# A hybrid attention layer on one core: the attention phase issued from a list of streams, and later values as transposed blocks

## The chip, the cores and the metric

The kernel runs on one core of one Trainium2 chip. The metric is the device time of one execution in microseconds (us); lower is better. The core's engines run side by side, each with its own instruction stream in a fixed order, and meet at semaphores: TensorE (PE, matrix products, with its weight loads shown as PEld), VectorE (DVE), ScalarE (ACT), GpSimd (POOL) and SyncE (SP), which issues the DMAs.

## The reference

One layer over x of 1024 frames by 1024 features, in float32, with RMS norms around each part:

```python
h = rmsnorm(x, g_mix_pre)
proj = h @ w_in          # fq, fk, fv, f_logit, cq, ck, cv
y_fox = forgetting_attention(fq, fk, fv, f_logit + b_fgt)       # 8 heads of 64
y_chk = chunked_relpos_attention(cq, ck, cv, rel_bias)          # 8 heads of 64
y = concat(rmsnorm(y_fox, g_fox_out), rmsnorm(y_chk, g_chk_out))
x = x + rmsnorm(y @ w_out, g_mix_post)
h = rmsnorm(x, g_mem_pre); mem_n = rmsnorm(mem, g_mem_kv)       # 256 memory tokens
x = x + rmsnorm(memory_cross_attention(h, mem_n, w_mq, w_mk, w_mv, w_mo), g_mem_post)
h = rmsnorm(x, g_ff_pre)
x = x + rmsnorm(square(relu(h @ w_ff1)) @ w_ff2, g_ff_post)
```

Forgetting attention ("f") is causal: query block i of 128 frames sees the i + 1 key blocks up to its own, with a bias from a cumulative sum of log forget gates. Chunked attention ("c") lets a chunk of 64 frames see itself and eight chunks before it, at most five key blocks per query block, with a relative-position bias.

## The kernel before

Every product is made from two parts of each float32 operand: a rounded part ("hi", made by ACT as a copy) and a remainder ("lo", made by DVE or POOL as a subtraction). `mm3` (lines 100 to 104) issues three matmuls for each product: hi x hi, lo x hi and hi x lo. Weights come by DMA into `wraw` (three buffers), and are split into `whi` and `wlo` (two buffers each) by `split_w` (lines 96 and 97).

The kernel has four stages: a prologue that normalises and transposes x into `hT` (two halves of 512 frames, hi and lo) and makes two groups of values; the attention phase; output projection and cross-attention; and the feed-forward part.

The attention phase goes through eight pairs of heads in the order c0, c1, f0, f1, f2, f3, c2, c3. For a pair:

- `project` (lines 261 to 295) makes the key block and then the query block: a stationary 128 x 128 weight block against 512 frames, 48 matmuls of 512 columns for each. Keys are written as `kd` (hi) and `kl` (lo, three buffers of the tag `klo`), and each half of 64 partitions is copied to the other half by a DMA (lines 281 and 283). Queries become `qs`.
- `values` (lines 224 to 235) makes the values of four heads: a stationary 128 x 128 block of `hT` against 256 columns of weights, 24 matmuls per block of frames, 192 for a group. Groups 0 and 1 are made in the prologue, groups 2 (heads f4 to f7) and 3 (c4 to c7) inside the attention phase.
- `attend` (lines 309 to 395), once per head, goes over four groups of two query blocks. It has scores (lines 338 to 342, pieces of up to 512 columns, in two PSUM banks of the tag `s`), the bias added and the row minimum taken by DVE in one instruction (line 344), the exponential by ACT (350), a reciprocal by DVE (352), the row scaled by POOL (353), transposes of the probabilities (379, two banks of `tr`), their split into `ph` by ACT (380) and `pl` by DVE (381), and four matmuls of 256 columns for every two key blocks (386 and 387, two banks of `pv`). The output leaves through `o2` and `ot` (391 and 392) and a DMA to DRAM (`od`).

The memory tokens are normalised during the fourth pair and transposed during the seventh. After the last pair come memory keys (`mem_keys`: 8 weight blocks, 24 matmuls of 256 columns each) and memory values (`mem_values`: 8 weight blocks, 12 matmuls of 512 columns each). Their weight remainders go alternately to DVE and POOL.

The prologue and the main part of the feed-forward stage are inside a block in which the written order is kept. Everything between, the attention phase included, is outside such a block: the compiler's scheduler, which estimates each instruction's duration and issues what is ready by the place in the text, makes the order. The code below is therefore not the order of issue; projections of the next pair and memory products appear between the steps of attention. Once made, each engine's order is fixed. A pool of 31 tiles of 4 KB per partition (`u4`) holds `hT` (16), queries, keys, values and later operands; a tile waits for the last reader of the one that it takes the place of.

Of the kernel before, what the change touches and what calls it, by code (L numbers as in the profile page):

```python
# [5 lines left out]

# [15 lines left out]
P = 128  # L22
# [11 lines left out]
def f(ap):  # L34
    return ap.bitcast(F32)


def layer(tc, out, t):
    nc = tc.nc
    ctx = ExitStack()  # L40
    with ctx:
        build(ctx, tc, nc, out, t)


def build(ctx, tc, nc, out, t):
# [16 lines left out]
    def u4(name, shape, dt=F32R):  # L62

        return up.tile(list(shape), dt, tag="u4", bufs=31, name=name)
# [83 lines left out]
    maskf = up.tile([P, P], F32, tag="u4", bufs=31, name="maskf")  # L148
# [31 lines left out]
    def load_x(b):  # L180
        tag = "sp" if b % 3 else "klo"
        xt = p1.tile([P, D], F32, tag=tag, bufs=5 if b % 3 else 3, name=f"x_{b}")
        nc.sync.dma_start(xt, t["x"][b * P:(b + 1) * P, :])
        return xt
# [6 lines left out]
    def bias_rows():  # L191

        rrow = p1.tile([8, 768], F32, tag="sp", bufs=5, name="rrow")
        rsrc = p1.tile([8, 256], F32, tag="sp", bufs=5, name="rsrc")
        nc.sync.dma_start(rsrc, t["rel_rev"])
        nc.vector.tensor_scalar(rrow[:, 511:767], rsrc, -1.0, None, op0=ALU.mult)
# [6 lines left out]
    def value_weights(g, raws=None, only=None):  # L203

        n = 264 if g == 0 else 256
        src = t["w_v0"] if g == 0 else t["w_v"][g - 1]
# [29 lines left out]

    def forget_gates():

        z, e, l, u = [p1.tile([8, S], F32, tag="sp", bufs=5, name=f"f{n}") for n in "zelu"]
        for g in range(2):  # L240
# [3 lines left out]
            nc.vector.tensor_scalar(z[:, g * HT:(g + 1) * HT], tr.rearrange("p a b -> p (a b)"),  # L244
                                    bfgt, None, op0=ALU.add)
        nc.vector.tensor_scalar(l, z, -1.0, None, op0=ALU.mult)
        nc.vector.tensor_tensor(l, l, z, op=ALU.min)
        nc.scalar.activation(e, l, AF.Exp)

        nc.vector.tensor_scalar(u, e, 1.0, None, op0=ALU.add)  # L250
        nc.scalar.activation(l, u, AF.Ln)
        nc.vector.scalar_tensor_tensor(e, u, 1.0, e, op0=ALU.subtract, op1=ALU.subtract)
        nc.scalar.activation(u, l, AF.Exp, scale=-1.0)
        nc.vector.tensor_tensor(e, e, u, op=ALU.mult)
        nc.vector.tensor_sub(e, e, l)
        nc.vector.scalar_tensor_tensor(e, z, 0.0, e, op0=ALU.min, op1=ALU.add)
        nc.vector.memset(u, 0.0)
        nc.vector.tensor_tensor_scan(l, e, u, 0.0, op0=ALU.add, op1=ALU.add)
        nc.sync.dma_start(cd, l)

    def project(kind, pr):

        qb = (0 if kind == "f" else 8) + pr
        kb = qb + 4
        qs = [u4(f"qs{kind}{pr}{a}", (P, S)) for a in range(2)]
        kd = [u4(f"kd{kind}{pr}{a}", (P, S)) for a in range(2)]
        kl = [p1.tile([P, S], F32R, tag="klo", bufs=3, name=f"kl{kind}{pr}{a}") for a in range(2)]  # L270
        step = 1 if kind == "f" else -1
        halves = [(slice(a * 64, a * 64 + 64), slice(64 - a * 64, 128 - a * 64)) for a in range(2)]
        wh, wl = load_w(t["w_qk"][kb], [P, KC, P])
        for th in range(2):
            ps = mm_tile([P, HT], f"k{kind}{pr}_{th}")
# [3 lines left out]
            for a, (own, oth) in enumerate(halves):  # L279
                nc.scalar.activation(kd[a][own, cs], ps[own], AF.Copy)  # L280
                nc.sync.dma_start(f(kd[a][oth, cs]), f(kd[a][own, cs]))
                nc.vector.tensor_sub(kl[a][own, cs], ps[own], f(kd[a][own, cs]))
                nc.sync.dma_start(f(kl[a][oth, cs]), f(kl[a][own, cs]))
        wh, wl = load_w(t["w_qk"][qb], [P, KC, P])
        for th in range(2):
            ps = mm_tile([P, HT], f"q{kind}{pr}_{th}")
            for kc in range(KC):
                mm3(ps, wh[:, kc, :], wl[:, kc, :], hT[th].hi(kc), hT[th].lo(kc), kc == 0, kc == KC - 1)
            pv = ps.rearrange("p (a b) -> p a b", b=P)[:, :, ::step]
            for a, (own, oth) in enumerate(halves):  # L290
                dst = qs[a].rearrange("p (a b) -> p a b", b=P)[:, th * 4:th * 4 + 4, :]
                nc.scalar.activation(dst[own], pv[own], AF.Copy, scale=-0.125)
                nc.vector.scalar_tensor_tensor(dst[oth], pv[own], -0.125, f(dst[own]),
                                               op0=ALU.mult, op1=ALU.subtract)
        return qs, kd, kl

    def head_bias(kind, h):
        bt = p1.tile([P, S], F32, tag="bias", bufs=2, name=f"bias{kind}{h}")
        if kind == "f":
            nc.sync.dma_start(bt, cd[h:h + 1, :].to_broadcast([P, S]))  # L300
        else:
            row = rd[h:h + 1, :]
            src = bass.AP(tensor=row.tensor, offset=row.offset, ap=[[1, P], [1, 640]])
            nc.sync.dma_start(bt[:, 0:640], src)
            nc.gpsimd.memset(bt[0:64, 0:64], BIG)
            nc.gpsimd.memset(bt[64:128, 576:640], BIG)
        return bt

    def attend(kind, pr, a, qs, kd, kl, vs):
        h = pr * 2 + a  # L310
        hv = (pr % 2) * 2 + a
        own = slice(a * 64, a * 64 + 64)
        oth = slice(64 - a * 64, 128 - a * 64)
        bt = head_bias(kind, h)
        kcol = pr if kind == "f" else 4 + pr
        step = 1 if kind == "f" else -1
        for g in range(4):
            nm = f"{kind}{h}g{g}"
            probs = []
            for i in (2 * g, 2 * g + 1):  # L320
                b0 = 0 if kind == "f" else max(0, i - 4)
                nk = (i + 1 - b0) * P
                k0 = b0 * P
                boff = 0 if kind == "f" else 640 - nk
                if g > 1 or i % 2 == 0:
                    wide = p1.tile([P, S], F32, tag="sp", bufs=5, name=f"sp{nm}{i}")
                sp = wide if g > 1 else wide[:, i % 2 * HT:(i % 2 + 1) * HT]
                mn = small.tile([P, 2], F32, tag="mn", bufs=6, name=f"mn{nm}{i}")
                if nk <= 512:
                    pieces = [(0, nk)]  # L330
                else:
                    first = 512 if nk - 512 >= 256 else nk - 256
                    pieces = [(0, first), (first, nk - first)]
                for j, (o, n) in enumerate(pieces):
                    w = max(n, 256)
                    ps = mm_tile([P, HT], f"s{nm}{i}{j}", "s")
                    last = kind == "f" and j == len(pieces) - 1
                    nc.tensor.matmul(ps[:, :w], qs[a][:, i * P:(i + 1) * P],
                                     kd[a][:, k0 + o:k0 + o + w], start=True, stop=False)
                    if last:  # L340
                        nc.tensor.matmul(ps[:, n - P:n], identb, mask, start=False, stop=False)
                    nc.tensor.matmul(ps[:, :w], qs[a][:, i * P:(i + 1) * P],
                                     kl[a][:, k0 + o:k0 + o + w], start=False, stop=True)
                    nc.vector.tensor_tensor_reduce(
                        out=sp[:, o:o + n], in0=ps[:, :n], in1=bt[:, boff + o:boff + o + n],
                        scale=1.0, scalar=3e38 if j == 0 else mn[:, 0:1],
                        op0=ALU.add, op1=ALU.min, accum_out=mn[:, j:j + 1])
                sm = small.tile([P, 2], F32, tag="sm", bufs=6, name=f"sm{nm}{i}")
                m = mn[:, len(pieces) - 1:len(pieces)]
                nc.scalar.activation(sp[:, :nk], sp[:, :nk], AF.Exp, scale=-1.0, bias=m,  # L350
                                     accum_out=sm[:, 0:1])
# [1038 lines left out]
```

## Time and profile before

| | |
|---|---|
| median of three runs | 1543.71 us (1543.68 to 1544.41) |
| the profiled execution | 1547.0 us, of which the span of its instructions is 1545.2 us |
| mean granted TensorE clock | 0.995 |
| first projection matmul, first output-projection matmul | 66.3 us, 567.8 us |
| HBM traffic over the span | 136 GB/s |

In the rows below, L338 is line 338 of the kernel, a name such as `sf7g<-kdf,qsf` says what is written and from what, with buffer numbers left out (`sf` and `sc` are scores, `ptrf` transposed probabilities, `pvf` the product with values), and a bracket at the end of a row tells for how long the engine stood idle before it and what released it. The duration of a matmul includes its way through the array, which overlaps the next one's, so durations of successive rows overlap.

### The profile page before, as it was taken

How to read it: one execution, taken by the hardware profiler on the slowest of the kernel's cores; microseconds unless marked ns; L12 is line 12 of the kernel's file. 1: busy time of each engine (PE TensorE's matmuls, PEld its weight loads, DVE VectorE, ACT ScalarE, POOL GpSimd, SP SyncE). 2: the span in 40 equal slices, each digit the busy share in tenths (PEclk: the TensorE clock that was granted, in tenths of full speed). 3: DMA queues.
4: the chain of work that ended last, by engine and by line, in shares of the span. 5: the costliest groups of instructions: out<-in, count | busy, mean ns of one | idle time of the engine just before them, and what ended most of it. 6: DMA issues, size and time to landing. Idle time of an engine off the chain costs nothing. (4 is left out here: it accounts for less than half of the span.)

```text
span 1545.2 us, 21983 instructions
## 1 busy us (share of the span) xinstructions
PE 1501.4 (97%) x7852; PEld 1270.6 (82%) x7852; DVE 938.2 (61%) x1640; ACT 789.8 (51%) x1405; POOL 374.2 (24%) x546
## 2 busy tenths in 40 slices
PE   8999999999999999989999998999999999999998
PEld 7978889789878987768888877888888888888886
DVE  6366574665466773775455468676455574746577
ACT  5356564565466675444444455555555544444442
POOL 4234351343234430121011320443233000000021
PEclk9999999999999999999999999999999999999999
DMA  5132140252222454453143154775444595535565
GB/s 215 50 95 66 52 113 23 66 156 64 56 65 90 121 169 139 160 184 106 55 154 105 55 177 168 242 246 181 153 155 150 189 384 194 171 114 192 198 245 191
DMA packets 83856, 220.71 MB, mean 143 GB/s; under 512 B 9865, under 2 KB 13969, under 8 KB 83746
## 3 DMA queue, kind: packets, MB, share of 16 engines
q1 hardware_dynamic: 83746, 219.30, 42.7%
q8 instruction: 62, 1.02, 0.3%
q14 instruction: 48, 0.39, 0.1%
HBM read 159.96 MB, written 50.91 MB: 136 GB/s over the span
## 5 line engine op out<-in xcount | busy, mean ns | idle before, releaser
L96 ACT ACTIVATE whi<-wraw 128x1024 fp32r<-128x1024 f32 x76 | 80.3, 1058 | 76.5 <-PE ym L104 19.0
L1117 ACT ACTIVATE whif<-ra 128x1024 fp32r<-128x1024 f32 x37 | 39.2, 1061 | 122.1 <-PE fy L103 62.6
L1119 DVE TENSOR_TENSOR wlof<-ra,whif 128x1024 fp32r<-128x1024 f32 x37 | 45.3, 1225 | 91.1 <-ACT whif L1117 91.1
L97 DVE TENSOR_TENSOR wlo<-wraw,whi 128x1024 fp32r<-128x1024 f32 x52 | 63.6, 1225 | 53.8 <-ACT whi L96 53.2
L1233 POOL TENSOR_SCALAR rf<-sf 128x1 f32<-128x1 f32 x8 | 8.3, 1035 | 326.5 <-ACT jf L1218 326.2
L102 PE MATMUL v<-whiv,hT_hi 128*128 128x256 f32 (+1 forms) x256 | 73.6, 287 | 1.0 <-DVE vs L235 1.0
L103 PE MATMUL v<-wlov,hT_hi 128*128 128x256 f32 (+1 forms) x256 | 73.2, 286 | 0.0
L104 PE MATMUL v<-whiv,hT_lo 128*128 128x256 f32 (+1 forms) x256 | 73.1, 286 | 0.0
L97 POOL TENSOR_TENSOR wlo<-wraw,whi 128x1024 fp32r<-128x1024 f32 x24 | 57.8, 2410 | 54.2 <-ACT whi L96 28.1
L102 PE MATMUL fx<-vhif,whif 128*128 128x512 f32 x168 | 65.4, 389 | 0.0
L104 PE MATMUL fx<-vhif,wlof 128*128 128x512 f32 x168 | 65.4, 389 | 0.0
L103 PE MATMUL fx<-vlof,whif 128*128 128x512 f32 x168 | 65.4, 389 | 0.0
L1007 POOL TENSOR_TENSOR sc<-wf,wf 128x512 f32<-128x512 f32 x14 | 22.8, 1627 | 144.4 <-DMA wf<-in_w_ff 125.0
L102 PE MATMUL yw<-whi,yT_hi 128*128 128x512 f32 x128 | 51.0, 403 | 2.2 <-ACT yw L605 1.6
L103 PE MATMUL ym<-wlo,oT_hi 128*128 128x512 f32 x128 | 50.9, 397 | 0.9 <-DVE wlo L97 0.8
L103 PE MATMUL mq<-h2T_lo,whi 128*128 128x512 f32 x128 | 51.5, 402 | 0.0
L102 PE MATMUL mq<-h2T_hi,whi 128*128 128x512 f32 x128 | 51.3, 402 | 0.1
L104 PE MATMUL mq<-h2T_hi,wlo 128*128 128x512 f32 x128 | 51.0, 399 | 0.0
L103 PE MATMUL yw<-wlo,yT_hi 128*128 128x512 f32 x128 | 50.6, 395 | 0.1
L102 PEld LDWEIGHTS v<-whiv,hT_hi 128*128 128x128 f32 x256 | 49.1, 192 | 1.5 <-DVE vs L235 1.2
L104 PE MATMUL yw<-whi,yT_lo 128*128 128x512 f32 x128 | 50.3, 393 | 0.0
L104 PE MATMUL ym<-whi,oT_lo 128*128 128x512 f32 x128 | 50.2, 395 | 0.0
(751 smaller groups left out, 5135.5 us busy)
## 6 DMA issues: line engine op xcount, KB each, us to landing
ra<-gd SPq DMA_DIRECT2D x56, 512.0 KB, 3.8
wg<-in_w_ff SPq DMA_DIRECT2D x56, 512.0 KB, 5.6
wf<-in_w_ff SPq DMA_DIRECT2D x38, 512.0 KB, 3.8
gd<-s SPq DMA_DIRECT2D x48, 256.0 KB, 2.1
wraw<-in_w_qk SPq DMA_DIRECT2D x16, 512.0 KB, 4.0
wraw<-in_w_mq SPq DMA_DIRECT2D x16, 512.0 KB, 4.3
wraw<-in_w_mo SPq DMA_DIRECT2D x16, 512.0 KB, 3.8
gd<-u SPq DMA_DIRECT2D x32, 256.0 KB, 2.1
```

The costliest lines, as they stand in the source:

```text
L96: nc.scalar.activation(hi, raw, AF.Copy)
L97: (lo_on or nc.gpsimd).tensor_sub(lo, raw, f(hi))
L102: nc.tensor.matmul(ps, lh, rh, start=start, stop=False, skip_group_check=more)
L103: nc.tensor.matmul(ps, lh, rl, start=False, stop=False, skip_group_check=more)
L104: nc.tensor.matmul(ps, ll, rh, start=False, stop=stop, skip_group_check=more)
L1007: eng.tensor_sub(sc[:, k1], r0[:, k0], r1[:, k0])
L1117: nc.scalar.activation(ah, ra, AF.Copy)
L1119: nc.vector.tensor_sub(al, ra, f(ah))
L1233: nc.gpsimd.tensor_scalar(r, ssf[b][:, 0:1], ssf[b][:, 1:2], EPS, op0=ALU.add, op1=ALU.add)
```

## The change

The attention phase becomes a block with a written order, and that order is computed while the program is built. `Flow` keeps one clock for PE and a time for each of DVE ("V"), ACT ("S"), POOL ("G") and SP's DMAs ("D"), with a duration for each instruction. Five streams are Python generators: each yields the PE time of its next step and a condition. At every point the first stream in the list whose condition holds gives its step; when none does, the clock goes on by 0.05 us. Instructions of the other engines are put in by the time at which they become ready, by level (0 first). `Tokens` count the buffers of each kind.

```python
    def past(self, at):
        return at + 0.2 <= self.now
...
    def run(self, streams):
        heads = [[g, next(g, None)] for g in streams]
        ...
            for h in heads:
                if h[1] and h[1][1]():
                    cost = h[1][0]
                    self.end = self.now + cost + 0.2
                    h[1] = next(h[0], None)
                    self.upto(self.now + cost)
                    ...
                    break
            else:
                ...
                self.upto(self.now + 0.05)
```

```diff
+    free = {k: Tokens(flow, n) for k, n in
+            dict(s=2, tr=2, pv=2, mm=2, sp=1, p=2, klo=4, bias=2, raw=2, w=0, u4=6).items()}
...
+        flow.run([value_steps(), turn_steps(), score_steps(), side_steps(), filler_steps(keep)])
```

The streams are: the products with values (one step for every two key blocks, 0.48 us); the transposes of probabilities; the scores (one piece for a step); side work (the forget gates, the transposes of values, the transposes of memory tokens); and the filler: for each pair the query block, from the fifth pair on the value block, and the key block, each in steps of three matmuls, and after the last pair memory keys and values.

```diff
+    def filler_steps(keep):
+        for n in range(8):
+            part = all_of(("qk", n), 12)
+            yield from project_steps("q", n, part)
+            if n > 3:
+                yield from project_steps("v", n, part)
+            yield from project_steps("k", n, part)
+        for _ in range(16):
+            free["u4"].give(flow.end)
+        yield from memory_steps(keep)
```

A projection may begin when its weight block is split and a bank and its output tiles are free; scores of a pair when its queries, keys and the key copies are complete:

```diff
+                yield (0.681, lambda: kc or there((what, n)) and free["mm"].ready() and
+                       (th or free["u4"].ready(u) and (what != "k" or free["klo"].ready(2))))
...
+                    def then(at, lo=lo, last=last, copy=copy, d=d, l=l):
+                        flow.load(at, lambda: copy(d), part, 2.3)
+                        flow.put("V", at, 0.7, lo, lambda end: (last(end), flow.load(
+                            end, lambda: copy(l), part, 2.3)), 1)
...
+            for what, m in (("u4", 2), ("klo", 1)):
+                for _ in range(m):
+                    free[what].give(flow.end)
```

The last three lines stand at the end of each head's scores.

Values of the last four pairs (f2, f3, c2, c3) are no longer made in groups of four heads. For each of these pairs a block of 128 weight columns is stationary against 512 frames, as for queries and keys; ACT copies the result out (`vt`), TensorE transposes it in blocks of 128, and ACT and DVE split the transposes into the value tiles:

```diff
+                for b in range(4):
+                    nc.tensor.transpose(tr[:, b, :], vt[n][:, th * HT + b * P:th * HT + (b + 1) * P], ident)
...
-        "w_v": a(np.stack([rows(cv[:, :256]), rows(fv[:, 256:]), rows(cv[:, 256:])])),
+        "w_v1": rows(cv[:, :256]),
+        "w_v": blocks(np.concatenate([fv[:, 256:], cv[:, 256:]], 1)),
```

`Stock` loads weight blocks in the order in which they are used and splits them as buffers come free: the rounded part on ACT, the remainder in two halves, on POOL for queries, keys and values and on DVE for memory keys and values:

```diff
+                vec = key[0] in ("mk", "mv")
...
+                def halves(at, key=key, eng="V" if vec else "G"):
+                    cost = 0.61 if eng == "V" else 1.3
```

Three blocks are loaded and two of them split within the prologue's loop, where the small loads for gates and biases also go:

```diff
+            if b == 2:
+                nc.sync.dma_start(bfgt, t["b_fgt"])
+                nc.sync.dma_start(gcol, t["g_heads"])
+                bias_rows(0)
+            if b == 4:
+                bias_rows(1)
+                stock.load(3)
+            if b == 6:
+                stock.split_now(2)
```

The tag `klo` has four buffers instead of three, and `u4` has 30 tiles instead of 31. All instructions after the attention phase are written as before.

More of the change, by code (lines that the diff above doesn't have):

```diff
@@ L35, in f, with __init__, ready, take @@
     return ap.bitcast(F32)
+class Tokens:
+    def __init__(self, flow, n):
+        self.flow, self.free = flow, [0.0] * n
+    def ready(self, n=1):
+        return len(self.free) >= n and sorted(self.free)[n - 1] <= self.flow.now
+    def take(self):
+        self.free.sort()
+        self.free.pop(0)
+    def give(self, at):
+        self.free.append(at)
+class Flow:
+    def __init__(self):
+        self.now = self.end = 0.0
+        self.free = dict.fromkeys(("V", "S", "G", "D"), 0.0)
+        self.waiting = {e: [] for e in self.free}
+        self.count, self.pumps = 0, []
+    def past(self, at):
+        return at + 0.2 <= self.now
+    def put(self, eng, at, cost, call, then=None, level=0):
+        self.count += 1
+        self.waiting[eng].append((level, at, self.count, cost, call, then))
+    def load(self, at, call, then=None, took=4.5):
+        self.put("D", at, 0.55, call, then and (lambda end: then(end + took)))
+    def chain(self, at, parts, then=None, level=2):
+        if not parts:
+            return then and then(at)
+        eng, cost, call = parts[0]
+        more = lambda end: self.chain(end + (2.5 if eng == "D" else 0.05), parts[1:], then, level)
+        self.put(eng, at, cost, call, more, level)
+    def upto(self, t):
+        while True:
+            best = None
+            for e, items in self.waiting.items():
+                if items:
+                    start = max(self.free[e], min(i[1] for i in items))
+                    if start <= t and (best is None or start < best[0]):
+                        best = (start, e)
+            if best is None:
+                break
+            start, e = best
+            item = min(i for i in self.waiting[e] if i[1] <= start)
+            self.waiting[e].remove(item)
+            _, _, _, cost, call, then = item
+            self.free[e] = start + cost
+            call()
+            if then:
+                then(start + cost + 0.05)
+        self.now = t
+    def run(self, streams):
+        heads = [[g, next(g, None)] for g in streams]
+        idle = 0
+        while any(h[1] for h in heads):
+            for pump in self.pumps:
+                pump()
+            for h in heads:
[4 more added lines that the diff above has]
+                    self.upto(self.now + cost)
+                    idle = 0
+                    break
+            else:
+                idle += 1
+                assert idle < 4000, "no step can be taken"
+                self.upto(self.now + 0.05)
+        self.upto(math.inf)
@@ L235, in values, with there @@
         nc.vector.tensor_sub(vs[kb // 2][:, kb % 2, :, 64:128], src, f(dh))
+    ORDER = (("c", 0), ("c", 1), ("f", 0), ("f", 1), ("f", 2), ("f", 3), ("c", 2), ("c", 3))
+    HALVES = [(slice(a * 64, a * 64 + 64), slice(64 - a * 64, 128 - a * 64)) for a in range(2)]
+    flow = Flow()
+    free = {k: Tokens(flow, n) for k, n in
+            dict(s=2, tr=2, pv=2, mm=2, sp=1, p=2, klo=4, bias=2, raw=2, w=0, u4=6).items()}
+    seen = {}
+    def there(*keys):
+        return all(flow.past(seen.get(k, math.inf)) for k in keys)
@@ L252, in forget_gates @@
[L252 to L273, printed above, removed]
+            parts.append(("V", 0.75, lambda g=g, tr=tr: nc.vector.tensor_scalar(
+                z[:, g * HT:(g + 1) * HT], tr.rearrange("p a b -> p (a b)"), bfgt, None, op0=ALU.add)))
@@ new lines, in done @@
+        def done(at):
+            seen["gates"] = at
+            for _ in range(4):
+                free["sp"].give(at)
+        for _ in range(2):
+            free["tr"].take()
+        flow.chain(flow.end, parts[:2], lambda at: [free["tr"].give(at) for _ in range(2)] and
+                   flow.chain(at, parts[2:], done))
+    bias, qs, kd, kl, vs2, probs, trs, pvs = {}, {}, {}, {}, {}, {}, {}, {}
+    heads = [(n, a) for n in range(8) for a in range(2)]
+    units = [(n, a, g) for n, a in heads for g in range(4)]
@@ new lines, in build, with __init__, pump, load @@
+    class Biases:
+        def __init__(self):
+            self.left = list(heads)
+        def pump(self):
+            while self.left and free["bias"].ready():
+                n, a = self.left[0]
+                kind, pr = ORDER[n]
+                if kind == "f" and not there("gates"):
+                    break
+                self.left.pop(0)
+                free["bias"].take()
+                h = pr * 2 + a
+                def load(n=n, a=a, kind=kind, h=h):
+                    bt = bias[n, a] = p1.tile([P, S], F32, tag="bias", bufs=2, name=f"bias{kind}{h}")
+                    if kind == "f":
+                        nc.sync.dma_start(bt, cd[h:h + 1, :].to_broadcast([P, S]))
+                    else:
+                        row = rd[h:h + 1, :]
+                        nc.sync.dma_start(bt[:, 0:640], bass.AP(tensor=row.tensor, offset=row.offset,
+                                                                ap=[[1, P], [1, 640]]))
+                def edges(bt):
+                    nc.gpsimd.memset(bt[0:64, 0:64], BIG)
+                    nc.gpsimd.memset(bt[64:128, 576:640], BIG)
+                if kind == "f":
+                    flow.load(flow.now, load, mark(("bias", n, a)))
+                else:
+                    flow.load(flow.now, load, lambda at, n=n, a=a: flow.put(
+                        "G", at, 0.3, lambda: edges(bias[n, a]), mark(("bias", n, a))))
@@ new lines, in key_steps @@
+    def key_steps(n, g):
+        kind = ORDER[n][0]
+        lo = [block_range(kind, i) for i in (2 * g, 2 * g + 1)]
+        kbs = list(range(lo[0], 2 * g + 2))
+        out = []
+        for c in range(0, len(kbs), 2):
+            slots = [(j, q) for j in range(2) for q in range(2)]
+            outside = lambda: [m for m, (j, q) in enumerate(slots) if not lo[q] <= kbs[c + j] <= 2 * g + q]
+            if outside():
+                slots = slots[2:] + slots[:2]
+            out.append((kbs[c:c + 2], slots, outside()))
+        return out
@@ L279, in project @@
[L279 to L307, printed above, removed]
@@ L397, in raw_tile @@
-    def raw_tile(name):
-        return wp.tile([P, D], F32, tag="wraw", bufs=3, name=name)
+                yield (0.681, lambda: kc or there((what, n)) and free["mm"].ready() and
+                       (th or free["u4"].ready(u) and (what != "k" or free["klo"].ready(2))))
+                if kc == 0:
+                    free["mm"].take()
+                    if th == 0:
+                        for _ in range(u):
+                            free["u4"].take()
+                        if what == "k":
+                            for _ in range(2):
+                                free["klo"].take()
+                    ps = mm_tile([P, HT], f"{what}{n}_{th}")
@@ new lines, in mem_norm, with mem_loads @@
+            store = lambda xt=xt, b=b: nc.sync.dma_start(md[b], xt)
+            flow.chain(flow.now + 6 + b, [("S", 1.1, square), ("G", 0.9, root), ("V", 1.3, scale), ("D", 0.55, store)],
+                       lambda at, b=b: [free["raw"].give(at) for _ in range(1 + b)] and seen.__setitem__(("md", b), at))
+    mem_in = []
+    def mem_loads():
+        for b in range(2):
+            xt = raw_tile(f"memn{b}")
+            nc.sync.dma_start(xt, md[b])
+            mem_in.append(xt)
+        seen["mem"] = flow.now + 6
```

538 lines of the change are left out of this document (369 added, 169 removed).

## The prediction

> **What bounds the kernel now.** I read the page first, then the busy times by stretch, then TensorE's rows in order of time, then the DMA issues.
>
> ```profile
> span 1545.2 us, 21983 instructions
> ...
> PE 1501.4 (97%) x7852; PEld 1270.6 (82%) x7852; DVE 938.2 (61%) x1640; ACT 789.8 (51%) x1405; POOL 374.2 (24%) x546
> ...
> PE 37%; DVE 1%; DMA 1%; issue 0%; ACT 0%; SPq 0%; DVEq 0%; POOLq 0%; POOL 0%; ACTq 0%
> ```
>
> TensorE (PE) sets the end; no other engine is near full. The change touches what runs from the first projection matmul (66.3) to the first output-projection matmul (567.8). In the busy times by stretch (length, then busy time of PE, PEld, DVE, ACT, POOL, then clock and DMA) that phase and three shorter pieces read:
>
> ```profile
> 66.30:567.80 501.50, 487.21 (x3048) 426.24 (x3046) 312.86 (x854) 300.14 (x624) 183.94 (x328) 1.00 0.30 87
> ...
> 350.00:400.00 50.00, 50.00 (x383) 47.27 (x382) 25.05 (x72) 22.89 (x52) 15.16 (x25) 1.00 0.17 51
> ...
> 446.00:463.00 17.00, 13.95 (x89) 11.06 (x88) 14.43 (x47) 13.07 (x30) 7.26 (x16) 1.00 0.35 96
> ...
> 568.00:575.00 7.00, 7.00 (x30) 5.73 (x29) 4.46 (x8) 3.65 (x6) 1.47 (x1) 0.85 0.24 78
> ```
>
> DVE is busy 62% of the phase, ACT 60%, POOL 37%. Busy PE hides gaps, because rows overlap. Undisturbed rows show what a matmul really takes (start, duration):
>
> ```profile
> 379.57 0.28 PE L103 MATMUL v<-wlov,hT_hi 128*128 128x256 f32 x1
> 379.69 0.28 PE L104 MATMUL v<-whiv,hT_lo 128*128 128x256 f32 x1
> ...
> 1400.28 0.39 PE L102 MATMUL fy<-vhif,whif 128*128 128x512 f32 x1
> 1400.51 0.39 PE L103 MATMUL fy<-vlof,whif 128*128 128x512 f32 x1
> ```
>
> From start to start a 512-column matmul takes 0.227 us and a 256-column one 0.120; the same reading gives 0.175 for 384 columns, 0.109 for a transpose, 0.039 for the mask. The phase's instructions by form are 960 of 512 columns, 1340 of 256, 128 of 384, 546 transposes, 64 masks and 8 small sums: 217.9 + 160.8 + 22.4 + 59.5 + 2.5 + 0.9 = 464.0 us of PE work in 501.5. So **37.5 us are gaps**, all that a better order can win here. They are unevenly spread. At 350 to 400, with value projections at hand to fill in, the same sum gives 49.2 of 50: 0.8 us of gaps. At 446 to 463, with attention alone, it gives 11.2 of 17:
>
> ```profile
> 448.68 0.50 PE L338 MATMUL sf7g<-kdf,qsf 128*128 128x512 f32 x1 [0.46 <-DVE mnf7g L344]
> ...
> 450.73 0.28 PE L386 MATMUL pvf7g<-phf7g,vs 128*128 128x256 f32 x1
> 451.85 0.44 PE L338 MATMUL sc4g<-kdc,qsc 128*128 128x384 f32 x1 [0.84 <-DVE mnc4g L344]
> ...
> 456.23 0.55 PE L379 MATMUL ptrf7g<-ident,spf7g 128*128 128x128 f32 x3 [0.85 <-POOL spf7g L353]
> ```
>
> PE stands, first in its order, at a score waiting for a bank that DVE has yet to reduce, or at a transpose waiting for POOL's normalised row, and no projection follows until 467.
>
> [...] By busy time the phase would have 14.3 us to win, by spacing 37.5; I go by spacing.
>
> **The change, part by part.**
>
> *PE work.* Removed: two value groups of 192 matmuls, 384 x 0.120 = 46.1 us. Added: four value blocks of 48 matmuls of 512 columns, 192 x 0.227 = 43.6, and 32 transposes, 3.5. Scores, turns, value products, q and k projections and memory are the same instructions. Net **+1.0 us**.
>
> *Other engines.* Copying a value block out costs ACT 8 copies of 0.60 and 8 splits of 0.60 against 16 of 0.38 (+3.4 us), DVE 8 x 0.69 against 16 x 0.42 (-1.2). The 8 memory-weight remainders that POOL had go to DVE (8 x 1.225 = +9.8 us in the last 80 us, where a memory block gives PE 2.9 us of work and DVE 1.2 + 0.4). Halving the other remainders adds at most 0.1 us x 20 on POOL. All this lies beside PE at 62, 60 and 37% busy; without that cover it would cost 12 us at most. I take nothing.
>
> *DMA and SP.* As many weight loads (512 KB), key copies and bias loads as before, issued in the list's order; SP waits in that order too, so a late key copy holds back weight loads and stores queued behind it. Phase traffic is 87 GB/s. Nothing for bytes.
>
> *The order.* Turn, score and value steps go ahead of projections, and whenever none is expected to be ready one projection step (three matmuls, 0.68 us) is taken. That attacks the gaps above directly. Query blocks now go before key blocks and there is a fourth buffer for key remainders; before, with three, a pair's keys could not be projected until the previous pair's first head let go of one. What is left of the 37.5 us I bound by rows: if all the phase is like 350 to 400, 0.84 x 465/50 = 8 us; if nothing improves, 37.5. The durations written into the list agree with the trace: copy 0.6 against 0.59, remainder 0.7 against 0.69, POOL row multiply 0.25 + 640/1150 = 0.81 against 0.804. One does not, the landing of key copies, written as 2.3:
>
> ```profile
> klc<-klc SPq DMA_DIRECT2D x16, 128.0 KB, 3.9
> ...
> klf<-klf SPq DMA_DIRECT2D x16, 128.0 KB, 2.6
> ```
>
> A pair's first score waits for them, PE stands in order at that score, and the filler queued behind it waits too: 1.6 us at three chunked boundaries and 0.3 at four others, 6 us if nothing covers. So **14 us** of gaps stay, nearer the fed stretch than the starved one, because the memory blocks (45 us) now follow as filler to the end.
>
> *Start.* Before, the value groups covered the wait for the first projection weights: PE has no gap of half a microsecond from 54 to 82. After, three blocks are loaded and two split during the prologue's value matmuls (ACT 2 x 1.06, POOL 4 x 1.2 us). Between -1 and +4 us; I take 0.
>
> *Hand-off.* Before, output-projection weights and head outputs were loaded and split under the memory values, and its first matmuls ran beside the last head. After, attention and memory are one written order, and part of this may come only after the last memory copy: first split 1.06 + 1.2, head outputs 4 x 0.72 on ACT, about 6 us, if not drawn ahead. That code outside a written order can be drawn into it shows at 54.09, where forget-gate transposes run amid the prologue's values. Between -2 (the last head's 3 us of gaps at 563 to 568 go) and +6. One slot fewer in the large pool (30 for 31) may delay a late load by one landing (3.8 us), or not. Together I take **+2 us**.
>
> The row at 568 to 575 shows a price tied to such gaps: clock 0.85, matmuls starting 0.43 us apart, after the thinly filled stretch before it. The Trainium skill (TensorE: Matmul & The Clock Gate, HAM oscillation) warns that idle gaps over about 3.4 us drop the clock to half. Here it fell though no single gap was that long, so a thin stretch suffices; by that rule an empty hand-off would add an estimated 1.7 us to my sum, which also stands within the range.
>
> *Sum.* -37.5 + 1.0 + 14 + 2 = -20.5 us. The profiled execution took 1547.0 us (span 1545.2, 1.8 around it); that gives 1526.5. The median of the runs is 1543.71, so **1523 us**.
>
> **The rivals.**
>
> 1. *Slower: the fine order is late at its waits.* 192 score pieces and 152 value steps each wait for DVE's or ACT's last result. Before, scores and value products have 29.7 us of the gaps ahead of them, 0.086 us for each of 344 places. The list allows 0.2 us for a result to arrive and then fixes the order; a result that comes later holds PE with the projection behind it. Zero gain lies at a residue of 34.5 us, 0.10 us per place; at 0.13 the residue is 45, the change +10, the time 1554. For: PE breaks its runs more often now, and DVE takes two more weight remainders per memory pair. Against: the durations agree, and the prior gaps are mostly where no filler was near.
>
> 2. *Starved at pair boundaries.* The next pair's key block needs two large tiles, which come free when a head's last score is issued. If filler runs out at the seven boundaries and the 446 stretch recurs there (5.9 us of gaps in 17, say half of that more than I counted), 7 x 2 = 14 us more: 1537. For: six large tiles are free at the start, four taken by each pair. Against: the fourth remainder buffer, and value blocks as filler from the fifth pair.
>
> 3. *Nearly all gaps close.* A residue of 4 us and no hand-off cost: 1511.
>
> 4. *The list doesn't set the order.* Code drawn into it displaces its steps, or it ends no better than the order before: residue 32 to 37, between 1541 and 1546.
>
> **How the numbers follow.** Forecast (1514 to 1533) 0.54; nearly all closes 0.08; starved 0.13; no better order 0.06; slower 0.19. 0.2%, 3.1 us, is about what a measurement can tell from no change. Faster by over that: the first three and a little of the fourth, 0.76; within 0.05; slower 0.19. The range reaches down to 1508, the third rival with the good ends of start and hand-off (1511 - 1 - 2), and up to 1547, leaving the worst of the first rival out; the forecast's own range is 1514 to 1533.
>
> **What would show it.** Right: the phase from the first projection matmul to the first output-projection matmul some 20 us shorter with the same work plus 1 us; projection steps in threes between score pieces throughout; no stretch like 446 to 463; DVE near 66% in the phase. Waits at pair boundaries name key copies if term two of the residue is right. Wrong: scores and value products held for DVE in hundreds of small waits (rival 1), runs of attention alone between pairs (rival 2), an empty PE or a clock under 1 at the first output-projection matmuls (hand-off), or time lost beyond 700 us (the missing slot).

## The result and the profile after

The changed kernel takes 1527.26 us in the median (1526.96 to 1528.19) against 1543.70 us: ratio 0.9894, 95% interval 0.9876 to 0.9911, that is 16.4 us less, where the sum forecast 20.5 (1523 us). The profiled executions are 18.8 us apart (1547.0 and 1528.19 us, spans 1545.2 and 1526.4).

The page of after, its first lines and the shares of the chain that ended last:

```profile
span 1526.4 us, 21650 instructions
...
PE 1492.2 (98%) x7692; PEld 1258.5 (82%) x7692; DVE 945.1 (62%) x1656; ACT 793.1 (52%) x1405; POOL 358.3 (23%) x558
...
PE 38%; DVE 1%; ACT 0%; DMA 0%; issue 0%; DVEq 0%; POOLq 0%; SPq 0%; POOL 0%; ACTq 0%
```

TensorE (PE) is the bound as before, and its busy time fell by only 9.2 us: with the span 18.8 us shorter, most of what went was time without a matmul, or time hidden in overlapping rows.

Busy time by stretch of after (length, then PE, PEld, DVE, ACT, POOL, clock, DMA share, GB/s): the phase from the first projection matmul to the first output-projection matmul, the piece that was starved before, and the hand-off:

```profile
65.70:548.20 482.50, 478.03 (x2890) 414.89 (x2889) 318.41 (x866) 300.04 (x619) 168.73 (x345) 1.00 0.32 94
...
446.00:463.00 17.00, 17.00 (x115) 15.54 (x114) 10.89 (x30) 10.73 (x23) 4.98 (x18) 1.00 0.14 36
548.00:555.00 7.00, 6.53 (x31) 4.83 (x30) 6.10 (x9) 4.72 (x8) 0.81 (x1) 1.00 0.80 256
```

The phase lasts 482.5 us instead of 501.5. Its matmuls are now 1152 of 512 columns, 960 of 256, 128 of 384, 584 transposes and 64 masks; at the spacings of the prediction 261.5 + 115.2 + 22.4 + 63.7 + 2.5 = 465.3 us. So 17.2 us of gaps are left of 37.5. At 446 to 463 there is no idle time, and the first 7 us of the hand-off run at full clock, where before they ran at 0.85. The thinnest 17 us of the phase now have 2.6 us of gaps (from 478.5); before, they had 6.4 (from 300.5). PE's waits in the phase are few, and this is the whole list (who waited for whom, us, times, longest):

```profile
PE mv L192 <- DVE wlomv L390: 1.3, 2, 1.1
PE sf3g L540 <- DVE mnf3g L546: 0.8, 1, 0.8
PE ptr L611 <- DVE vs L761: 0.6, 1, 0.6
PE sc7g L540 <- DVE mnc6g L546: 0.4, 1, 0.4
PE pv L648 <- DVE pl L617: 0.3, 1, 0.3
PE sf4g L540 <- DVE mnf4g L546: 0.3, 1, 0.3
PE sf6g L540 <- DVE mnf6g L546: 0.3, 1, 0.3
PE mk L193 <- DVE wlomk L390: 0.2, 1, 0.2
```

PE's rows of after in order of time (start, duration), from that piece:

```profile
448.42 0.42 PE L540 MATMUL sc5g<-kd,qs 128*128 128x384 f32 x1
448.68 0.34 PE L543 MATMUL sc5g<-kl,qs 128*128 128x384 f32 x1
448.85 0.40 PE L191 MATMUL v<-hT_hi,whiv 128*128 128x512 f32 x1
449.09 0.39 PE L192 MATMUL v<-hT_lo,whiv 128*128 128x512 f32 x1
449.32 0.39 PE L193 MATMUL v<-hT_hi,wlov 128*128 128x512 f32 x1
449.55 0.28 PE L647 MATMUL pv<-ph,vs 128*128 128x256 f32 x1
```

After a score piece one step of three value-block matmuls is taken, then the product that has become ready: no row has a wait in brackets.

Where the 18.8 us came from, by PE's first matmuls of each part:

| part | before | after | difference |
|---|---|---|---|
| to the first projection | 66.3 | 65.7 | -0.6 |
| attention phase | 501.5 | 482.5 | -19.0 |
| output projection, to the first memory query | 100.0 | 103.2 | +3.2 |
| memory queries, to the memory output | 73.4 | 72.1 | -1.3 |
| from there to the end | 804.0 | 802.9 | -1.1 |

### The profile page after: what moved, and what is told of

It reads as the page before. It is cut to its first block, busy times and chain, and to the rows that moved or that the text cites. A ratio compares the mean times of both kernels' runs of the same rounds, so it can differ in the third digit from the quotient of the medians.

```text
span 1526.4 us, 21650 instructions
## 1 busy us (share of the span) xinstructions
PE 1492.2 (98%) x7692; PEld 1258.5 (82%) x7692; DVE 945.1 (62%) x1656; ACT 793.1 (52%) x1405; POOL 358.3 (23%) x558
## 5 line engine op out<-in xcount | busy, mean ns | idle before, releaser
L617 DVE TENSOR_TENSOR pl<-ptr,ph 128x512 fp32r<-128x512 f32 (+1 forms) x152 | 91.7, 616 | 43.8 <-ACT ph L620 35.8
L620 ACT ACTIVATE ph<-ptr 128x512 fp32r<-128x512 f32 (+1 forms) x152 | 78.9, 540 | 56.4 <-PE ptr L611 51.1
L186 DVE TENSOR_TENSOR wlo<-wraw,whi 128x1024 fp32r<-128x1024 f32 x44 | 53.6, 1222 | 48.6 <-ACT whi L185 48.3
L647 PE MATMUL pv<-ph,vs 128*128 128x256 f32 x304 | 80.0, 287 | 0.0
L648 PE MATMUL pv<-pl,vs 128*128 128x256 f32 x304 | 78.8, 283 | 0.3 <-DVE pl L617 0.3
L185 ACT ACTIVATE whi<-wraw 128x1024 fp32r<-128x1024 f32 x44 | 46.3, 1058 | 50.0 <-PE ym L193 19.0
L648 PEld LDWEIGHTS pv<-pl,vs 128*128 128x128 f32 x304 | 57.6, 189 | 5.1 <-DVE pl L617 0.8
L647 PEld LDWEIGHTS pv<-ph,vs 128*128 128x128 f32 x304 | 57.3, 189 | 3.8
L191 PE MATMUL k<-hT_hi,whik 128*128 128x512 f32 x128 | 52.8, 412 | 0.0
L191 PE MATMUL q<-hT_hi,whiq 128*128 128x512 f32 x128 | 50.8, 397 | 0.0
```

Of the source, the lines that this page charges most:

```text
L185: nc.scalar.activation(hi, raw, AF.Copy)
L186: (lo_on or nc.gpsimd).tensor_sub(lo, raw, f(hi))
L191: nc.tensor.matmul(ps, lh, rh, start=start, stop=False, skip_group_check=more)
L617: flow.put("V", at, 0.7, lambda: nc.vector.tensor_sub(pl[:, live, :], tr[:, live, :], f(ph[:, live, :])), done)
L620: flow.put("S", flow.end, 0.6, lambda ph=ph, tr=tr, live=live: nc.scalar.activation(ph[:, live, :], tr[:, live, :], AF.Copy), split)
L647: nc.tensor.matmul(pv, v, ph[:, hs, :], start=c == 0 and half == 0, stop=False)
```

## The experiments

The theory: the gaps closed because projection steps are at hand at every score and value wait, in an order whose times fit the chip. Rivals: that the new value blocks, or the fourth buffer for key remainders, made the difference and the list is incidental; and, the prediction's first rival, that the fixed order loses at its waits. Ratios are to the kernel before on the same chip, with 95% intervals.

**e1, value blocks alone.** In the kernel before:

```diff
-                vs[g] = value_tiles(g)
-                for kb in range(TB):
-                    values(g, w, vs[g], kb)
+            if n > 2:
+                vb[n + 1] = value_block(n + 1)
```

> The kernel before, with the values of pairs f2, f3, c2 and c3 as transposed 128-column blocks, its order still made by the compiler's scheduler. Theory (the list's order closes the gaps, the new values only change 46.1 us of PE work into 47.1): 1541 to 1547 us, about 1545, gaps of the attention phase still 33 to 40 us. Rival (the smaller value blocks, one for each pair, are what feeds the starved stretches): 1530 to 1536 us, gaps down to 20 to 28 us.

1544.68 us, ratio 1.0011 (1.0001 to 1.0020): 0.9 us slower by the medians and 1.7 by the ratio, about what 1.0 us of extra PE work would give. By spacing its phase keeps 39.6 us of gaps:

```profile
66.20:570.65 504.45, 490.97 (x2888) 423.22 (x2886) 309.60 (x845) 301.27 (x625) 181.87 (x328) 0.99 0.30 87
```

So in the scheduler's order the value blocks alone win nothing, and that rival falls.

**e2, the list without value blocks.** In the kernel after:

```diff
-            if n > 3:
-                yield from project_steps("v", n, part)
+            if n in (4, 6):
+                yield from group_steps(n)
```

> The kernel after, with the values of the later pairs made as before, in two groups of four heads (192 matmuls of 256 columns each, as filler ahead of the key blocks of f2 and c2), and the list of streams kept. Theory (the order is the gain): 1525 to 1531 us, gaps of the phase 15 to 22 us. Rival (the value blocks are the gain): 1537 us or more. By PE work alone it should be 1 us shorter than the kernel after.

1540.46 us, ratio 0.9978 (0.9968 to 0.9987): only 3 us won. The theory missed, and the time is the rival's (1537 or more). With e1 this says that neither part is the gain by itself: in these forms the list needs the value blocks, and they need the list. Most of the loss sits in one place; the busy time of e2 there, PE's rows, and SP's next weight load:

```profile
300.00:325.00 25.00, 20.38 (x95) 15.85 (x94) 15.72 (x48) 15.62 (x34) 13.93 (x20) 0.86 0.61 192
```

```profile
305.59 0.36 PE L544 MATMUL sf4g<-kl,qs 128*128 128x256 f32 x1
308.38 0.44 PE L541 MATMUL sf4g<-kd,qs 128*128 128x384 f32 x1 [2.43 <-DVE mnf4g L547]
```

```profile
308.43 0.58 SPq L377 DMA_DIRECT2D wrawq<-in_w_qk  x1
```

Spacings leave 9.7 us of gaps in that stretch, against 1.2 in after. A value group needs both of its weight blocks, and so both pairs of split buffers, until its last matmul at 291; the key block behind it is split at 292, the memory norm, which takes all three load buffers, ends at 307, and the next query block is loaded at 308 and starts at 320.8. From 305, when the key block is done, until then f2 is scored with no projection between. A block for each pair holds one pair of split buffers for 11 us. So by this trace the value blocks matter by the buffers that they leave free, not by PE work; whether a value group placed otherwise would do was not tried.

**e3, buffers alone.** In the kernel before:

```diff
-        kl = [p1.tile([P, S], F32R, tag="klo", bufs=3, name=f"kl{kind}{pr}{a}") for a in range(2)]
+        kl = [p1.tile([P, S], F32R, tag="klo", bufs=4, name=f"kl{kind}{pr}{a}") for a in range(2)]
...
-        return up.tile(list(shape), dt, tag="u4", bufs=31, name=name)
+        return up.tile(list(shape), dt, tag="u4", bufs=30, name=name)
```

> The kernel before with four buffers for key remainders instead of three and 30 large tiles instead of 31, order by the compiler's scheduler. Theory (the order is the gain; the buffer alone lets the scheduler start a key block earlier, but it still orders by place in the text): 1538 to 1545 us. Rival (the third buffer was the starvation, the list is incidental): 1526 to 1532 us.

1540.18 us, ratio 0.9981 (0.9971 to 0.9990), within the theory's span: the scheduler gets some 3 us out of the two changes.

**e4, three buffers and keys first.** In the kernel after:

```diff
-            yield from project_steps("q", n, part)
             if n > 3:
                 yield from project_steps("v", n, part)
             yield from project_steps("k", n, part)
+            yield from project_steps("q", n, part)
...
-            dict(s=2, tr=2, pv=2, mm=2, sp=1, p=2, klo=4, bias=2, raw=2, w=0, u4=6).items()}
+            dict(s=2, tr=2, pv=2, mm=2, sp=1, p=2, klo=3, bias=2, raw=2, w=0, u4=6).items()}
```

> The kernel after with three buffers for key remainders, and key blocks before query blocks in the filler, both as in the kernel before; list and value blocks kept. Theory (the list is the gain, the buffer lets filler reach over the end of a pair): loses 3 to 8 us against after, 1530 to 1535. Rival (the buffer is most of the gain): 1538 to 1545 us, with runs of attention without projections between pairs.

1547.18 us, ratio 1.0024 (1.0014 to 1.0033): slower than either answer, with the whole gain gone. Busy time by stretch of e4, and the longest wait in each of these stretches, in PE's rows:

```profile
75.00:100.00 25.00, 20.33 (x91) 16.45 (x90) 18.06 (x37) 14.43 (x25) 8.62 (x11) 0.86 0.28 76
125.00:150.00 25.00, 22.13 (x114) 18.29 (x113) 13.31 (x38) 13.73 (x29) 8.93 (x15) 0.93 0.26 72
175.00:200.00 25.00, 22.51 (x110) 18.21 (x109) 11.95 (x31) 12.36 (x26) 8.18 (x14) 0.86 0.25 70
```

```profile
93.27 0.69 PE L540 MATMUL sc0g<-kd,qs 128*128 128x384 f32 x1 [4.46 <-DVE mnc0g L546]
...
143.63 0.44 PE L540 MATMUL sc2g<-kd,qs 128*128 128x384 f32 x1 [2.59 <-DVE mnc2g L546]
...
193.69 0.69 PE L540 MATMUL sf0g<-kd,qs 128*128 128x384 f32 x1 [2.33 <-DVE mnf0g L546]
```

At the first three pairs the filler is empty while a head is scored, 7.4, 5.5 and 6.3 us of gaps against at most 1.0 in after, and the clock falls to half for some microseconds each time, which makes the matmuls after the wait longer too. In the busy times by stretch around these waits, the clock is the third number from the end:

```profile
88.80:90.80 2.00, 0.01 (x1) 0.00 (x0) 1.97 (x2) 1.82 (x3) 0.05 (x1) 1.00 0.00 0
90.80:97.60 6.80, 4.33 (x13) 3.25 (x13) 5.29 (x19) 3.00 (x9) 4.70 (x7) 0.50 0.28 82
145.40:148.80 3.40, 3.40 (x12) 2.60 (x11) 2.32 (x13) 2.38 (x7) 2.46 (x7) 0.50 0.51 157
193.20:200.00 6.80, 6.16 (x20) 4.41 (x21) 4.10 (x19) 3.92 (x11) 4.72 (x8) 0.50 0.24 77
```

The Trainium skill (TensorE: Matmul & The Clock Gate, HAM oscillation) gives idle gaps over about 3.4 us as the cause of such a fall. The trace agrees in part: the first fall comes with the wait of 4.46 us, though already 2.0 us into it, and the other two come where the longest waits are 2.59 and 2.33 us. So a gap of that length is not needed here, nor was it in the kernel before, where the clock fell at 566.7 us and the longest wait just ahead was 0.75 us.

**e5, three buffers, queries first.** Only the last line of e4's edit.

> The kernel after with three buffers for key remainders, queries still first. Theory (what e4 lost is the block at the head of the filler: a key block that must wait for a buffer keeps every later projection back, and a query block ahead of it gives PE work for that time; the large tiles already hold key blocks back until the pair before has scored its first head): 1527 to 1531 us, no stretch of 25 us with over 4 us of gaps before 470. Rival (the fourth buffer is the cause): 1538 us or more, with the stretches at 75, 125 and 175 us of e4.

1529.02 us, ratio 0.9907 (0.9893 to 0.9922), as expected. The phase has 17.2 us of gaps, as in after. So while queries go first, these runs show no gain from the fourth buffer. e4 and e5 differ in the order of the blocks alone, so with three buffers keys first cost 18 us. The list's conditions say how: the key block at the head of the filler waits for a buffer of the pair in hand, and the query block, behind it, waits too. Keys first with four buffers was not run.

**e6, no margin.**

```diff
-        return at + 0.2 <= self.now
+        return at <= self.now
```

> The kernel after with the 0.2 us that a result is given to arrive taken out of the list's conditions. Theory of late waits (each of 344 score and value places is near its limit): 1534 to 1545 us, gaps of the phase up from 17 to 25 us or more. Rival (PE has room, and the list's durations are a little long anyway): 1525 to 1530 us.

1527.04 us, ratio 0.9895 (0.9879 to 0.9912), 15.8 us of gaps: no difference, as the rival had it.

**e7, key copies landing later in the list.** Both landing times of the key copies:

```diff
-                        flow.load(at, lambda: copy(d), part, 2.3)
+                        flow.load(at, lambda: copy(d), part, 3.9)
...
```

> The kernel after with the landing time of key copies in the list raised from 2.3 to 3.9 us. Theory of the prediction (late key copies cost up to 6 us at the pair boundaries): 1521 to 1525 us. Rival (PE does not wait for key copies at all, as the trace of after names none): 1526 to 1529 us.

1535.12 us, ratio 0.9948 (0.9933 to 0.9963): 8 us slower than after, and slower than either answer. The DMA issues of after in the phase explain why nothing could be won:

```profile
kd<-kd SPq DMA_DIRECT2D x32, 128.0 KB, 2.2
kl<-kl SPq DMA_DIRECT2D x32, 128.0 KB, 2.2
```

The copies land in 2.2 us; 3.9 was how those of the chunked remainders went in the order before. Why the later time costs 8 us is only partly seen: gaps between 500 and 575 us, where the last value products and the memory values meet the work drawn in from the next stage, rise from 5.7 to 13.0 us, with two falls to half clock; the first pair's scores add 2. What puts the order wrong there stays open.

**e8, three repairs.** Squares of the memory norm over the gain's tile, with the gain loaded again behind them; memory-value remainders half on DVE, half on POOL; output-projection banks of two tags:

```diff
-                junk = p1.tile([P, D], BF16, tag="ph", bufs=2, name=f"junkm{b}")
-                nc.scalar.activation(junk, xt, AF.Square, scale=1.0 / 32.0, accum_out=ss)
+                nc.scalar.activation(g, xt, AF.Square, scale=1.0 / 32.0, accum_out=ss)
...
+                    flow.put("V", at, 0.61, lambda: self.lo(key, nc.vector, 0), last, 2)
+                    flow.put("G", at, 1.3, lambda: self.lo(key, nc.gpsimd, 1), last, 2)
...
-                    ps = mm_tile([P, HT], f"yw{th}{g}{nh}{b}")
+                    ps = mm_tile([P, HT], f"yw{th}{g}{nh}{b}", "mm" if b % 2 else "s")
```

The waits of after that the first one is aimed at, in ACT's rows:

```profile
262.96 1.06 ACT L804 ACTIVATE junkm<-mem 128x1024 bf16<-128x1024 f32 x1 [2.06 <-PE pv L647]
...
269.80 1.06 ACT L804 ACTIVATE junkm<-mem 128x1024 bf16<-128x1024 f32 x1 [2.35 <-PE pv L647]
```

> The kernel after with three repairs of waits that its trace names: the memory norm's squares written over the gain's tile instead of a probability tile (ACT stood 4.4 us for those at 261 and 268 us), memory-value remainders half on DVE and half on POOL at the same time (PE stood 1.3 us at 536), and output-projection banks of two tags instead of one (5 us of waits for ACT and DVE at 549 to 613 us). Theory: 2 + 1 + 4 us, 1518 to 1523 us. Rival (each only moves the wait to the next release): 1525 us or more.

1525.06 us, ratio 0.9885 (0.9870 to 0.9900), not clear of after, and at the edge of the rival's answer. The norm's repair took some 2 us of gaps from 250 to 275 (2.5 to under 1). The remainders on two engines won nothing (4.3 us of gaps at 525 to 550, against 3.0). With four banks the output projection ran 9 us faster (101.3 to 92.4 us from its first to its last matmul), and then, in PE's rows:

```profile
647.20 2.31 PE L216 MATMUL tr_h<-ident,yw 128*128 128x128 f32 x8 [5.77 <-DVE h2T_lo L230]
651.39 1.97 PE L216 MATMUL tr_h<-ident,yw 128*128 128x128 f32 x8 [1.88 <-DVE h2T_lo L230]
```

DVE has the sums and gains of the later blocks ahead of the remainders of these transposes. The wait moved, and cost a stretch at half clock.

**e9 and e12, durations too short.** The durations of DVE, ACT and POOL in the list times 0.5 (e9) and 0.7 (e12):

```diff
-        self.waiting[eng].append((level, at, self.count, cost, call, then))
+        self.waiting[eng].append((level, at, self.count, cost * (1.0 if eng == "D" else 0.5), call, then))
```

> The kernel after with the durations of DVE, ACT and POOL instructions in the list halved, so that the list expects results too early. Theory (the gain needs the durations to fit, since PE's order is fixed and a score or value step put too early holds the projection behind it): gaps of the phase up from 17 to 35 us or more, 1540 to 1555 us. Rival (streams and their priorities are enough, filler at hand does the rest): 1526 to 1532 us.

> The kernel after with the durations of DVE, ACT and POOL in the list at 0.7 of what they were; the trace's own durations are within some 5% of the list's for copies and remainders. How much error does the list bear? If the loss grows with the error from the first (e9: 99 us over after at 0.5): about 1580 us. If PE's room and the 0.2 us margin take up a part (DVE is busy 62 to 66% of the phase, so at 0.5 the list believes it a third busy and at 0.7 under half): 1535 to 1560 us. Under 1532 would say that the durations matter only where they are grossly wrong.

e9: 1625.79 us, ratio 1.0541 (1.0521 to 1.0561). e12: 1567.27 us, ratio 1.0158 (1.0141 to 1.0175). e9 is far over both its answers, and e12 lies between its two. So 30% too short costs 40 us against after, and 50% costs 99; smaller errors were not run. The two costliest of PE's waits of e9 in the phase:

```profile
PE pv L648 <- DVE pl L617: 14.4, 42, 0.8
PE pv L647 <- ACT ph L620: 11.6, 15, 1.0
```

In all, PE has 106 waits of 58 us in the phase, where after has 9 of 4 us. Value products put before their probabilities are split, and transposes put before POOL's row is there, hold PE with ready projections behind them: the prediction's first rival, where its condition is made true. Scores, which it named too, cost less.

**e10, coarse filler.** Steps of twelve matmuls for the first six pairs. As in e2, the tile of the transposed memory tokens is also taken only at their first transpose.

```diff
-                yield (0.681, lambda: kc or there((what, n)) and free["mm"].ready() and
...
+                if kc % (4 if n < 6 else 1) == 0:
+                    yield (2.724 if n < 6 else 0.681, lambda: kc or there((what, n)) and free["mm"].ready() and
...
```

> The kernel after with projection steps of twelve matmuls (2.7 us) instead of three (0.7 us) for the first six pairs. Theory (DVE and ACT idle while a long step runs, attention falls behind and uses up the filler before the pair's end): 1530 to 1538 us. Rival (PE is as full with long steps): 1526 to 1529 us.

1540.08 us, ratio 0.9984 (0.9973 to 0.9994): slower than the theory's span, and all but 2 us of the gain gone. Between 100 and 200 us the gaps are some 10 us, in after under 2; PE's waits there are all scores waiting for DVE, 5.5 us in five waits. That fits the theory, but its steps are not shown one by one.

**e11, two repairs.** The norm as in e8, and four banks for the first half of the output projection alone:

```diff
+                    ps = mm_tile([P, HT], f"yw{th}{g}{nh}{b}", "mm" if g or b % 2 else "s")
```

> The kernel after with the memory norm's squares over the gain's tile, as in e8, and four banks for the first half of the output projection alone (the half that ACT evacuates); memory-value remainders and the second half, which DVE evacuates, as in after. Theory (e8 won 9 us in the output projection and lost 11 to DVE's queue ahead of the transposes after it; the first half needs no DVE): 2 us from the norm and 2 to 4 from the banks, 1520 to 1524 us. Rival (whatever PE wins there is waited for at the same transposes): 1525 us or more.

1522.18 us, ratio 0.9868 (0.9853 to 0.9882), as expected: 20 us under before and, by the ratios, some 4 under after, the two intervals overlapping a little. From the first output-projection matmul to the first memory query it takes 98.6 us, less than after's 103.2 and before's 100.0. It has the lowest median here.

One combination was not run: value blocks, the fourth buffer and queries first together, in the order of the compiler's scheduler. What the list itself is worth beside these three is therefore not measured; e9, e10 and e12 show that the durations in it and the length of its steps matter.

## Why the prediction came out as it did

The direction, the place and most of the size were right; by the medians the sum was 4 us too good. Of these, 1.7 us lie in its terms: the profiled executions are 18.8 us apart, where the sum says 20.5 (gaps 3.2 more, PE work 0.3 more, start 0.6 less, hand-off 1.2 less). The other 2.4 us lie in the execution that the sum starts from: the profiled one of before took 3.3 us more than the median, that of after 0.9 more.

- *What bounds it.* Right: the gaps by spacing were there to be won. 20.3 us went from the phase's gaps, more than the 14.3 us that busy time would have allowed.
- *PE work, +1.0 us.* Measured 465.3 against 464.0, so +1.3, and e1 alone costs about that.
- *Other engines at nothing.* DVE is busy 66% of the phase as forecast; PE's waits for weight remainders in the phase come to 1.5 us, at the memory keys and values. So taking nothing was nearly right.
- *Gaps left, 14 us.* This is the term that was mis-sized: 17.2. The fed stretch's rate was a fair floor: outside three thin pieces the phase has 9.8 us of gaps in 409 us, 1.2 for every 50 us, against 0.8 there. But key copies, put at up to 6 us, cost nothing: in the new order they land in 2.2 us and no wait of PE names them. In their place stand the three pieces, 7.4 us. One is the memory norm's squares (2.5 us at 250 to 275, of which e8 won some 2 back); they take a probability tile that the list does not count, so ACT stood still with other work queued behind. One is the end of the memory values, where the next stage's splits compete (2.4 us at 525 to 548). At 475 to 500 (2.5 us) no wait is longer than 0.4 us, and the cause stays open. That these came near the 6 us put down to key copies is luck.
- *Start, 0.* -0.6 us.
- *Hand-off, +2.* +3.2 us in the output projection, then 2.4 back later, so +0.8. (The pieces of its worst case, 1.06 + 1.2 + 4 x 0.72, add to 5.1 us, not to about 6.) The first copies and head outputs were drawn ahead, as assumed, and the half clock at 568 went away; but the stage's two banks are now waited for (5.2 us for ACT and DVE, 2.2 before).
- *Rivals.* The first did not come because the list's durations fit; e9 and e12 show it is as dear as feared and dearer when they do not, and e6 that the 0.2 us of margin does not matter. The second's mechanism is real as well: e2 and e4 are starved kernels, by weight buffers and by remainder buffers where the prediction named large tiles. In after the query block ahead of the key block, and value blocks of one pair, keep work at hand.
- What the prediction did not see is how little the parts pay by themselves, in the forms tried: value blocks alone +0.9 us, buffers alone -3.6, the list without value blocks -3.3. The list with value blocks and queries first, but three remainder buffers (e5), wins 14.2 of the 16.4 us (differences of medians).

## What to carry to other kernels

Sum matmul spacings, not busy time, to see what an order can win, and look for stretches with nothing to fill waits. A written order needs three things at once: filler that no buffer can block, steps short enough not to delay the latency chain, and durations taken from a trace: 30% too short cost more than twice the whole gain. After it, look at what the freed engine queues up on next: as far as e8 and e11 can tell, more banks helped only in the half that did not load the engine of the next wait.

## What was not expected of the hardware

A lack of work on PE is paid twice: in e4 a single wait of 4.46 us is followed by matmuls at half clock until 97.6 us, and the stretch's mean clock is 0.86. Waits of 2.59 and 2.33 us in thin stretches brought the same fall. The median landing of the 128 KB copies of key remainders went from 3.9 us (chunked heads) and 2.6 us (forgetting heads) before to 2.2 us after, in another order of issue; which part of that order does it was not separated.
